# A hybrid decoder block on one core: gates computed ahead of the branch projections, the projections in seven block products, and a written instruction order

## The chip, the core and the metric

One core of a Trainium2 chip runs the whole block in one launch. The metric is device time in microseconds (us). TensorE (PE) multiplies, VectorE (DVE), ScalarE (ACT) and GpSimd (POOL) work elementwise, SyncE (SP) issues most DMAs.

## The reference

1024 tokens and 16 meta tokens, width 1024, fp32. Three mixers read one normalised input; their outputs are projected, gated and merged, then come an output projection, a residual and a squared-ReLU MLP. What is computed after the mixers:

```python
g = sigmoid(gates).reshape(b, l, 3, 1024)          # gates = h @ w_in[:, 9216:12288]
merged = (g[:, :, 0] * (ret @ w_branch[0]) + g[:, :, 1] * (diff @ w_branch[1])
          + g[:, :, 2] * (conv @ w_branch[2]))
x = x + merged @ w_out
u = square(relu(rms_norm(x, norm2_w) @ w_up))      # 1024 -> 4096
return x + u @ w_down                              # then the final rms_norm
```

## The kernel before

Tokens lie along the free dimension, channels on the 128 partitions. A matrix product works on tiles of 128 output channels (f) by 512 tokens (a half, j). Each fp32 operand is split into a high part hi (a cast to fp32r) and a rest lo = x - hi (`split`, L135 and L136); each 128-deep step of a product is three matmuls: hi.hi, hi.lo, lo.hi (`kstep`, L161 to L163; `product`, L858 to L860). The hi part of a weight is copied on ACT, the lo part is subtracted on POOL.

**Mixers.** Retention, differential attention and the convolution are woven together; each leaves its output, by tiles of channels, in DRAM: `rT`, `dT`, `cT`.

**Gates and branches (L690 to L740).** For each of the three branches, in the order conv, attention, retention: the 8 operand tiles are loaded and split into the slots that the mixers left (L714). For each f, the gate columns of `w_in` are multiplied with H, the normalised input, scaled (L250, DVE) and put through a sigmoid (L704, ACT); two gates run ahead of the branch product. The product of the branch with its `w_branch` tile takes 8 steps of three matmuls a half; DVE multiplies it with the gate and adds it to the merged tile M (L736 to L739). Then M is split.

**Output projection (L758 to L776).** For each half and f: 24 matmuls, the residual is added (L766), the sum stored to DRAM, squared on ACT (L769) and summed over f on DVE (L773). Ones times that sum (L775) gives the sum of squares for all partitions; `rstd_from` (L188 to L192) makes the scale R2 of it with two ACT and three DVE operations.

**Up and down projections (L777 to L1014).** Here products are made of seven block products (Strassen-Winograd). A pair of f tiles, split in K and in N, is a 2 x 2 of blocks; the right operand's seven blocks are B11, B21, T1 = B12 - B11, B22, T2, T3 and T4, each kept as hi and lo in eight and six buffers of SBUF (`opnd`). The weight's seven left blocks are made from four loaded blocks by four DVE sums a pair (`comb`, L825) and split on ACT and POOL. Two pairs (four f) run together in `block_products`: seven times 2 x 4 x 3 = 24 matmuls, with the copies of finished banks on ACT (L869). The right blocks of the up projection come from X2 by `normalise` (L908) and `sums` (L929). The results U are squared ReLUs (L966, L967), their seven blocks go to DRAM. The down projection sums over 32 tiles of U in blocks of 16, 16, 16 and 8 by pairs; `right_ops` (L1006) loads seven blocks ahead of each and splits them, alternating POOL and DVE; `down_use` adds the residual on POOL (L1012) and the product on DVE (L1013). The last four tiles of U go through plain matmuls in `last_down` with the final norm, the tail.

The order of instructions on each engine is planned by the framework from dependencies and priorities; weights have high priority. Within an engine everything runs in that order. SP issues every load and nearly every store, also in order.

Memory: one stack of pools. `cp`, `xp` (tags C and R) and `sm` stay to the end; the others are closed behind the output projection, and the pools of the up and down projections take their place.

Of the kernel before, what the change touches and what calls it, by code (L numbers as in the profile page):

```python
# [12 lines left out]
F32 = mybir.dt.float32  # L13
# [58 lines left out]
def trunk_kernel(ctx: ExitStack, tc, x, w_in, w_branch, w_out, w_up, w_down, w_down2, w_down3, vecs, lam_in, consts, y):  # L72
    nc = tc.nc
    PSUM = bass.MemoryType.PSUM
    early = ExitStack()
    cp = ctx.enter_context(tc.tile_pool(name="cp", bufs=1))
    xp = ctx.enter_context(tc.tile_pool(name="xp", bufs=1))
    sm = ctx.enter_context(tc.tile_pool(name="sm", bufs=6))
    ap = early.enter_context(tc.tile_pool(name="ap", bufs=1))
    wp = early.enter_context(tc.tile_pool(name="wp", bufs=3))  # L80
    sp = early.enter_context(tc.tile_pool(name="sp", bufs=1))
    ps = early.enter_context(tc.tile_pool(name="ps", bufs=1, space=PSUM))
# [4 lines left out]
    def slot(tag, shape, dt=F32):  # L87
        uid[0] += 1
        return (xp if tag in ("C", "R") else sp).tile(shape, dt, tag=tag, bufs=SLOTS[tag], name=f"{tag}{uid[0]}")
# [176 lines left out]
    dT = [dram([P, SEQ]) for _ in range(KT)]  # L266
    cT = [dram([P, SEQ]) for _ in range(KT)]
    rT = [dram([P, SEQ]) for _ in range(KT)]
# [78 lines left out]
    def diff_attn(h, ops):  # L347
# [102 lines left out]
        nc.gpsimd.dma_start(out=dT[h], in_=o32)  # L450
# [19 lines left out]
    def conv_out(f, u):  # L470
# [3 lines left out]
        for c0, w in CH_TOK:  # L474
# [8 lines left out]
            if c0 != META:  # L483
                nc.gpsimd.dma_start(out=cT[f], in_=yt)
# [49 lines left out]
    def ret_gate(h, yt):  # L534
        for z in range(2):
            wt = weights(w_in[G_RG + 2 * h + z])
            for c0, w in CH_TOK:
# [8 lines left out]
                if c0 != META:  # L546
                    nc.gpsimd.dma_start(out=rT[2 * h + z], in_=yt[z])
# [142 lines left out]
    turns[:] = TURNS  # L690
    last_sig = [None]
    M = [None] * KT
    otags = ["Q"] * 4 + ["B"] * 4 + ["S"] * 2 + ["A"] * 6
    for br, src in ((2, cT), (1, dT), (0, rT)):
        def gate(f):
            if f >= KT:
                return None
            wt = weights(w_in[G_GATE + br * KT + f])
            out = []
            for c0, w in CH_TOK:  # L700
                pt = gemm(wt, H, c0, w)
                gt = slot("t2", [P, 512])
                scaled(gt, pt, c0, w)
                sig = a.activation(out=gt, in_=gt, func=AF.Sigmoid)  # L704
                last_sig[0] = sig
                out.append(gt)
            return out
        O = []

        def operands(ks):  # L710
            for k in ks:
                oh = slot(otags[2 * k], [P, SEQ], F32R)
                ol = slot(otags[2 * k + 1], [P, SEQ], F32R)
                nc.sync.dma_start(out=f32(ol), in_=src[k])  # L714
                for j in range(2):
                    c = slice(j * 512, (j + 1) * 512)
                    split(f32(ol[:, c]), oh[:, c], ol[:, c])
                O.append((oh, ol))

        gq = [gate(0)]  # L720
        operands(range(0, 4))
        gq.append(gate(1))
        operands(range(4, 8))
        for f in range(KT):
            gts = gq[f]
            wt = weights(w_branch[br * KT + f])
            if M[f] is None:
                M[f] = slot("C", [P, SEQ])
            if f == KT - 1:
                pts = gemm2(wt, O)  # L730
            else:
                pts = [gemm(wt, O, i * 512, 512) for i in range(2)]
            for i, pt in enumerate(pts):
                mc = M[f][:, i * 512:(i + 1) * 512]
                if br == 2:
                    v.tensor_tensor(out=mc, in0=pt, in1=gts[i], op=ALU.mult)  # L736
                else:
                    v.tensor_tensor(out=gts[i], in0=pt, in1=gts[i], op=ALU.mult)
                    v.tensor_tensor(out=mc, in0=mc, in1=gts[i], op=ALU.add)  # L739
            gq.append(gate(f + 2))  # L740


    with tc.issue_after(getattr(last_sig[0], "ins", last_sig[0])):
        a.preload_act_table_set("natural_log_exp_and_others")
    MO = []
    for k in range(KT):
        mh = slot("H", [P, SEQ], F32R)
        ml = slot("H", [P, SEQ], F32R)
        split(M[k], mh, ml)
        MO.append((mh, ml))  # L750

    X2 = [None] * KT
    xd = [dram([P, SEQ]) for _ in range(KT)]
    R2 = slot("R", [P, SEQ])
    for i in range(2):
        c = slice(i * 512, (i + 1) * 512)
        acc = None
        for f in range(KT):  # L758
            wt = weights(w_out[f])
            if X2[f] is None:  # L760
                X2[f] = slot("C", [P, SEQ])
            uid[0] += 1
            raw = wp.tile([P, HW], F32, tag="raw", name=f"xr{uid[0]}")
            nc.sync.dma_start(out=raw, in_=x[:, f, META + i * 512:META + i * 512 + 512])
            pt = gemm(wt, MO, i * 512, 512)
            v.tensor_tensor(out=X2[f][:, c], in0=pt, in1=raw, op=ALU.add)  # L766
            nc.sync.dma_start(out=xd[f][:, c], in_=X2[f][:, c])
            sq = slot("t2", [P, 512])
# [39 lines left out]
    def row_ops(srcs, cols):  # L808
# [18 lines left out]
        with tc.high_priority():  # L827
            a11 = [load(s[0]) for s in srcs]
            for p in range(n):
                op(0, a11[p])  # L830
# [317 lines left out]
```

## Time and profile before

| what | value |
|---|---|
| median of 3 runs | 2437.56 us (2434.89 to 2437.66) |
| the profiled execution, its own time | 2437.59 us |
| its span, first to last instruction | 2435.8 us |
| mean granted TensorE clock | 0.986 of full speed |
| bytes moved by DMA | 209.56 MB, 86 GB/s |

Times in the trace count from the span's start. A matmul's recorded duration overlaps the next one's, since they are pipelined; the rate of a stretch is read from the number of matmuls in it. The granted clock 1.00 is 2.4 GHz, 0.50 is 1.2 GHz.

### The profile page before, as it was taken

What the parts mean: (1) busy time and instruction counts of PE and PEld (TensorE: products, weight loads), DVE (VectorE), ACT (ScalarE), POOL (GpSimd) and SP (SyncE); (2) the same over time, 40 slices, a digit from 0 to 9 for tenths busy, and PEclk for the clock granted to TensorE, in tenths of its full rate; (3) what the DMA queues carried; (4) which work ended last, traced back from release to release, by engine and by line L of the source; (5) the groups of instructions that cost most, each with busy time, mean ns of one, the idle gap of its engine ahead of it and who ended that gap; (6) DMA issues with size and microseconds to landing.
All of it is one profiled execution on the core that took longest, in us unless ns stands there. A gap on an engine that the chain in (4) does not pass through costs nothing. (4 is left out here: it accounts for less than half of the span.)

```text
span 2435.8 us, 32151 instructions
## 1 busy us (share of the span) xinstructions
PE 2338.4 (96%) x11994; PEld 2021.5 (83%) x11994; DVE 1393.6 (57%) x2639; ACT 956.7 (39%) x1867; POOL 961.2 (39%) x768
## 2 busy tenths in 40 slices
PE   8999999999999999999999999998599999989897
PEld 7999999999999989988888888876478887767777
DVE  7776777776765676671122232244676668656545
ACT  6554554554543333341131131132333335344344
POOL 2233223222222211222222222233765557898894
PEclk9999999999999999999999999999799999999999
DMA  3111111111111111131131131134245356434221
GB/s 136 35 53 44 44 53 44 44 53 44 44 53 39 54 56 53 52 128 56 44 120 44 49 116 48 48 96 153 71 139 173 131 163 251 177 117 156 96 95 70
DMA packets 96300, 209.56 MB, mean 86 GB/s; under 512 B 10640, under 2 KB 14864, under 8 KB 93456
## 3 DMA queue, kind: packets, MB, share of 16 engines
q1 hardware_dynamic: 92688, 194.92, 23.1%
q0 software_dynamic: 3456, 12.58, 1.3%
q8 instruction: 94, 1.54, 0.3%
q14 instruction: 62, 0.51, 0.1%
HBM read 158.71 MB, written 48.76 MB: 85 GB/s over the span
## 5 line engine op out<-in xcount | busy, mean ns | idle before, releaser
L136 POOL TENSOR_TENSOR wlo<-raw,whi 128x512 fp32r<-128x512 f32 x270 | 367.6, 1363 | 1071.5 <-ACT whi L135 997.1
L161 PE MATMUL pmm<-H,whi 128*128 128x512 f32 (+3 forms) x1704 | 598.1, 353 | 9.7 <-ACT H L196 7.1
L163 PE MATMUL pmm<-H,wlo 128*128 128x512 f32 (+3 forms) x1704 | 598.5, 352 | 3.6 <-POOL wlo L136 3.6
L162 PE MATMUL pmm<-H,whi 128*128 128x512 f32 (+3 forms) x1704 | 598.3, 352 | 2.2 <-DVE H L197 2.2
L136 POOL TENSOR_TENSOR w<-raw,w 128x512 fp32r<-128x512 f32 (+1 forms) x224 | 310.3, 1396 | 152.5 <-ACT w L135 151.8
L858 PE MATMUL pb<-op,w 128*128 128x512 f32 x840 | 331.2, 398 | 39.4 <-ACT w L135 31.8
L161 PEld LDWEIGHTS pmm<-H,whi 128*128 128x128 f32 x1704 | 320.6, 189 | 39.6 <-ACT H L196 7.1
L163 PEld LDWEIGHTS pmm<-H,wlo 128*128 128x128 f32 x1704 | 320.9, 188 | 32.8 <-POOL wlo L136 6.6
L135 ACT CAST whi<-raw 128x512 fp32r<-128x512 f32 x272 | 168.7, 621 | 453.7 <-PE pmm L162 154.9
L162 PEld LDWEIGHTS pmm<-H,whi 128*128 128x128 f32 x1704 | 321.1, 189 | 30.0 <-DVE H L197 3.2
L859 PE MATMUL pb<-op,w 128*128 128x512 f32 x840 | 332.6, 396 | 8.9 <-DVE op L136 6.9
L860 PE MATMUL pb<-op,w 128*128 128x512 f32 x840 | 324.6, 396 | 12.3 <-POOL w L136 12.1
L135 ACT CAST w<-raw 128x512 fp32r<-128x512 f32 (+1 forms) x224 | 131.2, 595 | 319.5 <-PE pb L860 176.2
L858 PEld LDWEIGHTS pb<-op,w 128*128 128x128 f32 x840 | 161.4, 192 | 78.0 <-ACT w L135 35.1
L825 DVE TENSOR_TENSOR raw<-raw,raw 128x512 f32<-128x512 f32 (+1 forms) x128 | 144.4, 1150 | 105.5 <-POOL w L136 52.0
L860 PEld LDWEIGHTS pb<-op,w 128*128 128x128 f32 x840 | 160.0, 191 | 52.7 <-POOL w L136 19.6
L859 PEld LDWEIGHTS pb<-op,w 128*128 128x128 f32 x840 | 161.0, 192 | 43.7 <-DVE op L136 7.6
L250 DVE TENSOR_TENSOR t<-pmm,R 128x512 f32<-128x512 f32 (+2 forms) x60 | 36.8, 619 | 85.5 <-PE pmm L163 85.4
L380 ACT ACTIVATE B<-B,nb 128x144 f32<-128x144 f32 (+3 forms) x64 | 50.7, 792 | 85.5 <-DVE nb L379 85.2
L704 ACT ACTIVATE t<-t 128x512 f32<-128x512 f32 x48 | 30.4, 633 | 123.2 <-DVE t L250 122.1
L135 ACT CAST op<-op 128x512 fp32r<-128x512 f32 x106 | 58.6, 619 | 37.9 <-DMA op<-d 37.6
L371 PE MATMUL ps<-A,Q 128*128 128x256 f32 (+6 forms) x224 | 72.3, 327 | 0.3 <-DVE mx L374 0.3
(336 smaller groups left out, 4301.3 us busy)
## 6 DMA issues: line engine op xcount, KB each, us to landing
raw<-w_in SPq DMA_DIRECT2D x192, 256.0 KB, 2.5
d<-C SPq DMA_DIRECT2D x122, 256.0 KB, 3.0
op<-d SPq DMA_DIRECT2D x21, 1024.0 KB, 5.7
raw<-w_up SPq DMA_DIRECT2D x64, 256.0 KB, 2.9
raw<-w_down SPq DMA_DIRECT2D x56, 256.0 KB, 2.8
raw<-w_branch SPq DMA_DIRECT2D x48, 256.0 KB, 2.6
d<-C POOLq DMA_DIRECT2D x16, 512.0 KB, 3.0
raw<-w_out SPq DMA_DIRECT2D x32, 256.0 KB, 3.2
```

The source lines that it names most:

```text
L135: a.copy(out=hi, in_=src)
L136: (eng or v).tensor_tensor(out=lo, in0=src, in1=f32(hi), op=ALU.subtract)
L161: nc.tensor.matmul(pt, lhsT=hi[:, s], rhs=xh[:, c0:c0 + w], start=start, stop=False)
L162: nc.tensor.matmul(pt, lhsT=hi[:, s], rhs=xl[:, c0:c0 + w], start=False, stop=False)
L163: nc.tensor.matmul(pt, lhsT=lo[:, s], rhs=xh[:, c0:c0 + w], start=False, stop=stop)
L250: v.tensor_tensor(out=out, in0=pt, in1=R[:, c0:c0 + w], op=ALU.mult)
L371: nc.tensor.matmul(sps[:, 0:cw], lhsT=q[m][:, qc], rhs=kk[m][:, c], start=True, stop=False)
L380: a.activation(out=pt, in_=pt, func=AF.Exp, scale=slope, bias=nb, accum_out=st[:, m:m + 1])
L825: v.tensor_tensor(out=dst, in0=x0, in1=x1, op=o)
L858: nc.tensor.matmul(pt, lhsT=w[0][:, s], rhs=b[0][:, k], start=first, stop=False, skip_group_check=True)
L859: nc.tensor.matmul(pt, lhsT=w[0][:, s], rhs=b[1][:, k], start=False, stop=False, skip_group_check=True)
L860: nc.tensor.matmul(pt, lhsT=w[1][:, s], rhs=b[0][:, k], start=False, stop=k == nk - 1, skip_group_check=True)
```

## The change

The 24 gate tiles are computed ahead of all branches, in one loop that the framework still orders; the sigmoids are stored to DRAM (`GD`) by POOL's queue. In the same loop, from the third gate tile on, the sums T1 to T4 of the branch outputs are made and stored to DRAM (`TD`), and the first four right blocks of the first branch are loaded and split.

From there on the work is a list of steps: 42 for the branches (three branches, two quads of four f, seven products), 16 for the output projection, 56 for up and 56 for down. Each step has a load (issued three steps ahead), a preparation of its weights (two steps ahead), its matmuls in two parts, and an evacuation of each part; further tables place the splitting of right blocks, loads and stores at steps. The main loop at the end writes all engines' instructions in this order, and the framework keeps it.

Per step a `Quad` runs one of the seven products for two pairs: 24 matmuls. Weight lo parts go three in four to POOL, one to DVE (`WLO`). Right blocks are split by `build`: copies three in four on ACT, one on DVE; lo parts three in four on DVE, one on POOL. Right blocks of the next set are loaded in steps 1 to 7 and split in steps 3 to 9 counted from the last quad of the current set (`turn_over`). In the output projection lo parts alternate between POOL and DVE, and the sum of squares moves from DVE to POOL. The merging of branches and the residual adds of the down projection alternate between POOL and DVE. The up projection begins with products 1 and 2 of its first two quads; its seven right blocks follow one a step.

Pools stand on two stacks. On the left `cp`, and above it the mixers' pools (with tag C), which close ahead of the gates and give way to `pa` (eight right-block buffers) and `mp` (weights). On the right H, R, the temporaries and the gates' weights, which close ahead of the steps and give way to `pb` (six buffers) and `mq` (rings: kept banks 6, gates 3, X 16). The eight PSUM banks are one ring from the first step on. `last_down` keeps its work. The core of the diff:

```diff
-    early = ExitStack()
+    mixers, gates = ExitStack(), ExitStack()
...
+    RING = {"raw": 10, "w": 5, "t": 6, "g": 3, "k": 2, "X": 16}
...
-    for br, src in ((2, cT), (1, dT), (0, rT)):
-        def gate(f):
...
-            if f == KT - 1:
-                pts = gemm2(wt, O)
-            else:
-                pts = [gemm(wt, O, i * 512, 512) for i in range(2)]
...
+    for n, (br, f) in enumerate((br, f) for br, _ in BR for f in range(KT)):
+        wt = weights(w_in[G_GATE + br * KT + f])
+        for c0, w in CH_TOK:
+            pt = gemm(wt, H, c0, w)
+            gt = slot("t2", [P, 512])
+            scaled(gt, pt, c0, w)
+            last_sig = a.activation(out=gt, in_=gt, func=AF.Sigmoid)
+            nc.gpsimd.dma_start(out=GD[br][:, f, c0 - META:c0 - META + w], in_=gt)
+        if n >= 2 and sums_todo and n != 14:
+            branch_sums(*sums_todo.pop(0))
+        if n == 14:
...
+        def op(self, i, p, src):
+            w = temp("w", [P, 2, 512], F32R)[:, :, 0:self.nk * P]
+            a.copy(out=w[:, 0], in_=src)
+            lo_part("w", self.lo_engines, src, w[:, 0], w[:, 1])
...
+    def build(src, oh, ol, key="set"):
+        e = pick(key + "c", (a, a, a, v))
+        if e is a:
+            a.copy(out=oh, in_=src)
+        else:
+            v.tensor_copy(out=oh, in_=src)
+        lo_part(key + "l", (v, v, v, G), src, oh, ol)
...
+            at(fetch, L + i + 1, load)
+            at(work, L + i + 3, split_op)
...
+                if sb is not None:
+                    v.tensor_tensor(out=sb, in0=pt, in1=sb, op=ALU.add)
...
+                    v.tensor_tensor(out=g, in0=pt if sb is None else sb, in1=g, op=ALU.mult)
+                    pick("m", (G, v)).tensor_tensor(out=M[f, j], in0=M[f, j], in1=g, op=ALU.add)
+
+            for s, (r, j) in ((-1, (0, 0)), (2, (0, 1)), (4, (1, 1)), (5, (1, 0))):
+                at(fetch, L + s, lambda r=r, j=j, fn=gate_load: fn(r, j))
...
+    mid = {S0 + 9: lambda: token_scale(0), E0: lambda: token_scale(1)}
...
+    at(work, E0 + 1, lambda: up_t1(range(2)))
+    at(work, E0 + 2, lambda: up_t1(range(2, 4)))
+    at(work, E0 + 3, lambda: plain_op("B22", range(4)))
+    at(work, E0 + 4, lambda: up_sum("T2", (1, 1), (1, 1), (0, 1)))
+    at(work, E0 + 5, lambda: up_sum("T3", (0, 0), (1, 1), (0, 0)))
+    at(work, E0 + 6, lambda: up_sum("T4", (1, 0), (1, 0), (1, 1)))
...
+    with tc.manual_schedule():
+        for s in range(-LL, N + 2):
+            now[0] = s
+            if 0 < s <= N:
+                steps[s - 1][3](1)
+            for fn in soon.get(s, ()):
+                fn()
+            if 0 <= s + LP < N:
+                steps[s + LP][1]()
+            if 0 <= s < N:
+                steps[s][2](0)
+                if s in mid:
+                    mid[s]()
+                steps[s][2](1)
+                steps[s][3](0)
+            for fn in work.get(s, ()):
+                fn()
+            for fn in fetch.get(s, ()):
+                fn()
+            if 0 <= s + LL < N:
+                steps[s + LL][0]()
```

## Rows read from the trace of the kernel before

**Rows 1.** The page: busy us, share of the span and instructions.

```profile
PE 2338.4 (96%) x11994; PEld 2021.5 (83%) x11994; DVE 1393.6 (57%) x2639; ACT 956.7 (39%) x1867; POOL 961.2 (39%) x768
```

**Rows 2.** Stages: length, PE, PEld, DVE, ACT, POOL busy, PE clock, DMA share, GB/s.

```profile
0.00:1076.20 1076.20, 1064.40 (x6484) 993.36 (x6485) 752.13 (x1903) 512.05 (x1077) 270.45 (x275) 1.00 0.16 56
1076.20:1608.60 532.40, 532.40 (x2304) 431.57 (x2303) 138.34 (x197) 118.19 (x191) 127.02 (x99) 1.00 0.19 67
1608.60:1725.10 116.50, 98.06 (x390) 71.98 (x388) 45.07 (x50) 36.03 (x61) 44.92 (x33) 0.97 0.48 152
1725.10:2063.10 338.00, 315.61 (x1345) 257.57 (x1346) 245.19 (x263) 129.28 (x231) 213.29 (x135) 0.95 0.43 148
2063.10:2388.80 325.70, 293.58 (x1249) 235.85 (x1248) 184.63 (x178) 140.57 (x266) 288.93 (x215) 0.97 0.36 128
2388.80:2435.80 47.00, 34.37 (x229) 31.13 (x227) 28.20 (x52) 20.61 (x44) 16.54 (x14) 0.88 0.26 90
```

**Rows 3.** Busy time in three single stretches, same columns.

```profile
1725.00:1735.00 10.00, 5.00 (x10) 2.98 (x10) 10.00 (x7) 1.60 (x4) 8.96 (x6) 0.50 0.14 54
1800.00:2000.00 200.00, 200.00 (x884) 165.59 (x883) 132.77 (x151) 71.83 (x126) 107.77 (x74) 1.00 0.46 154
2065.00:2070.00 5.00, 4.89 (x21) 4.05 (x22) 4.54 (x4) 3.62 (x8) 5.00 (x4) 1.00 1.00 409
```

**Rows 4.** Waits of PE, 1608.6 to 2388.8: us in total, times, longest.

```profile
PE pb L858 <- ACT w L135: 31.8, 6, 7.4
PE pb L860 <- POOL w L136: 12.1, 13, 3.9
```

**Rows 5.** Timeline where the up stage begins: start, us, instruction, idle before.

```profile
1717.86 1.13 PE L775 MATMUL po<-t,onesr 128*128 128x512 f32 x2 [2.17 <-DVE t L773]
1724.48 1.64 DVE L908 SCALAR_TENSOR_TENSOR C<-C,vec,R 128x512 f32<-128x512 f32 x1
1725.09 0.80 PE L858 MATMUL pb<-op,w 128*128 128x512 f32 x1 [6.11 <-ACT w L135]
```

**Rows 6.** Lines 136 and 478: ns shortest/median/longest, first and last start.

```profile
L136 POOL TENSOR_TENSOR op<-op,op x42: 1272/1732/1822, 2035.3 to 2257.2; 128x512 fp32r<-128x512 f32 x42
L136 DVE TENSOR_TENSOR op<-op,op x42: 673/1744/1803, 2036.4 to 2257.7; 128x512 fp32r<-128x512 f32 x42
L478 DVE TENSOR_SCALAR C<-C,vec x16: 481/488/1514, 124.9 to 789.7; 128x512 f32<-128x512 f32 x16
```

**Rows 7.** Timeline of POOL and DVE, 1734 to 1770, neighbours merged.

```profile
1737.17 13.05 POOL L136 TENSOR_TENSOR op<-t,op 128x512 fp32r<-128x512 f32 x1 [3.20 <-ACT op L135]
1746.60 2.48 DVE L929 TENSOR_TENSOR C<-C 128x512 f32<-128x512 f32 x4
1756.31 10.15 POOL L136 TENSOR_TENSOR op<-C,op 128x512 fp32r<-128x512 f32 x6
1756.82 3.48 DVE L929 TENSOR_TENSOR C<-C,C 128x512 f32<-128x512 f32 x2
```

**Rows 8.** Groups of instructions, whole span: count, busy us, mean ns, idle before.

```profile
L869 ACT COPY t<-pb 128x512 f32<-128x512 f32 x96 | 55.7, 581 | 2.6 <-PE pb L860 2.6
L1013 DVE TENSOR_TENSOR C<-pb,t 128x512 f32<-128x512 f32 x48 | 32.2, 684 | 31.8 <-POOL t L1012 21.9 <-PE pb L860 9.7
```

**Rows 9.** The page: DMA issues, count, KB each, us to landing.

```profile
op<-d SPq DMA_DIRECT2D x21, 1024.0 KB, 5.7
raw<-w_up SPq DMA_DIRECT2D x64, 256.0 KB, 2.9
```

**Rows 10.** Instructions on the DRAM buffers: issuing a DMA on POOL, ns.

```profile
L450 POOL DMA_DIRECT2D d<-C x8: 533/573/573, 168.4 to 803.3; - x8
```

**Rows 11.** Busy time of L136 alone in the down stage: DVE, POOL.

```profile
2063.10:2388.80 325.70, 64.43 (x45) 219.55 (x163) 0.97 0.36 128
```

**Rows 12.** Groups of instructions in the down stage, columns as rows 8.

```profile
L825 DVE TENSOR_TENSOR raw<-raw,raw 128x512 f32<-128x512 f32 (+1 forms) x62 | 76.2, 1254 | 61.2 <-POOL w L136 30.8 <-DMA raw<-w_down 30.0
L1012 POOL TENSOR_TENSOR t<-t,C 128x512 f32<-128x512 f32 x48 | 68.2, 1422 | 0.0
```

More of the change, by code (lines that the diff above doesn't have):

```diff
@@ L743, in trunk_kernel @@
[L743 to L768, printed above, removed]
-            a.activation(out=sq, in_=X2[f][:, c], func=AF.Square)
-            if acc is None:
-                acc = sq
-            else:
-                v.tensor_tensor(out=acc, in0=acc, in1=sq, op=ALU.add)
-        ssq = bank("o")
-        nc.tensor.matmul(ssq, lhsT=ones, rhs=acc, start=True, stop=True)
-        rstd_from(ssq, D, R2[:, c], slot("t2", [P, 512]))
@@ L854, in product @@
-    def product(pt, w, b, nk, more):
-        for k in range(nk):
-            s = slice(k * P, (k + 1) * P)
-            first = k == 0 and not more
-            nc.tensor.matmul(pt, lhsT=w[0][:, s], rhs=b[0][:, k], start=first, stop=False, skip_group_check=True)
-            nc.tensor.matmul(pt, lhsT=w[0][:, s], rhs=b[1][:, k], start=False, stop=False, skip_group_check=True)
-            nc.tensor.matmul(pt, lhsT=w[1][:, s], rhs=b[0][:, k], start=False, stop=k == nk - 1, skip_group_check=True)
@@ new lines, in trunk_kernel, with acc_bank, at @@
+    gates.close()
+    pb = ctx.enter_context(tc.tile_pool(name="pb", side="right", **reuse))
+    mq = ctx.enter_context(tc.tile_pool(name="mq", side="right", **reuse))
+    p8 = ctx.enter_context(tc.tile_pool(name="p8", space=PSUM, **reuse))
+    def acc_bank():
+        uid[0] += 1
+        return p8.tile([P, 512], F32, tag="b", bufs=8, name=f"pb{uid[0]}")
+    LP, LL = 2, 3
+    steps = []
+    work = {}
+    fetch = {}
+    soon = {}
+    def at(table, s, fn):
+        table.setdefault(s, []).append(fn)
@@ new lines, in trunk_kernel, with load, split_op, merged @@
+    for i, name in enumerate(ORDER[4:]):
+        def load(name=name):
+            open_op(SET, name, 4, False)
+            nc.sync.dma_start(out=f32(SET[name][1]), in_=right_src(2, name))
+        def split_op(name=name):
+            for k in range(4):
+                build(f32(SET[name][1][:, k]), SET[name][0][:, k], SET[name][1][:, k])
+        at(fetch, -1, load)
+        at(work, 2 + i, split_op)
+    MO = {}
+    KO = (0, 1, 2, 3, 4, 6, 5, 7)
+    def merged(f, js):
+        if f not in MO:
+            MO[f] = opnd(True, [P, 2, SEQ])
+        for j in js:
+            build(M[f, j], MO[f][:, 0, half(j)], MO[f][:, 1, half(j)])
@@ L955, in store, with use @@
                 if p0 <= pair < p0 + n:
[L956 to L961 removed]
+                    put(UD[b][name][:, pair - p0, :], src)
+        def use(p, r, j, pt, sb):
+            u = U[r, j] = temp(FIRST_U[pair] if pair < 4 and (r, j) == (0, 0) else "X", [P, 512])
             if sb is None:
```

567 lines of the change are left out of this document (333 added, 234 removed).

## The prediction

> **What bounds the kernel now.** I began with the page's busy shares: TensorE is busy 96% of the span, no other engine over 57% [rows 1]. An average hides stages, so next came the busy time by stage [rows 2]. The reader should see two halves. Up to 1608.6 us PE never idles (532.40 of 532.40 us in the gate and branch stage): there, only fewer or shorter matmuls can help. From 1608.6 to 2388.8 us PE is short of work: 18.4 us idle in the output projection, 22.4 in the up stage, 32.1 in the down stage.
>
> Busy time is not the right measure of what each stage could do, so I count matmuls. 2304 in 532.4 us is 231 ns each in the gate and branch stage; in a full stretch of the up stage 884 in 200 us is 226.6 ns (two at an edge may count twice) [rows 2, 3]. At 226.6 ns the 384 of the output stage would take 87.2 us (it takes 116.5), the 1344 of the up stage 304.5 (338.0) and the 1176 of the down stage 266.5 (325.7): 29.3, 33.5 and 59.2 us, 122 us in all, are idle time or half clock. The half clock is real but small: after a wait of 6 us the clock stood at 0.50 (1.2 GHz) for a whole 10 us stretch [rows 3, 5].
>
> What PE waits for is a weight operand: the hi half from ACT (31.8 us), whose copy waits for a block sum on DVE, or the lo half from POOL (12.1) [rows 4]. So DVE and POOL are behind the stalls. Neither is full on its own (DVE 184.6 and POOL 288.9 of 325.7 us in the down stage [rows 2]), but they get in each other's way. The same lo subtraction takes 1.27 us at least on POOL and 1.73 in the middle; on DVE 0.67 and 1.74 [rows 6]. When both queue, six POOL ops take 10.15 us and two DVE ops 3.48: they alternate, 1.69 to 1.74 us a pair [rows 7]. A DVE op alone with a queue behind it takes 0.62 (four in 2.48); so I charge 0.62 us for a DVE op with two SBUF inputs and 1.07 for a POOL op, against one common account, the **pair**. DVE ops that read PSUM stay at 0.684 us on average, with POOL 89% busy [rows 2, 8], and are not charged. The account can also be won outright by one side: while DVE ran some twenty such ops in a row, one POOL op lasted 13.05 us [rows 7].
>
> **The change, part by part.**
>
> *Fewer products.* Three branches now take 8 x 2 x 8 x 3 = 384 matmuls each; seven products of 4 x 4 x 3 = 48 make 336. 144 fewer. The gates stay 1152 at 231 ns, 266.2 us. The branch products take the form of the up stage (one bank, weights and operands in the same layout), so I price them at its 226.6 ns: 1008 x 0.2266 = 228.4 us; at 231 ns it would be 4.4 us more. Together 494.6 instead of 532.4: **37.8 us** less, on the path, because PE is full there.
>
> *Gates first.* Each of 48 sigmoid halves is now stored by POOL's DMA queue and read back by SP; 48 more POOL stores carry the branch sums. A POOL DMA issue takes 0.57 us [rows 10], 96 of them 55 us, beside 48 lo subtractions at 1.27, 61 us: 116 of 266 us. The 48 new DVE sums are 30 us. The cover is 266 us of gate matmuls that need none of it; without the cover the 55 us would delay lo halves one for one. I charge nothing.
>
> *Hand-over.* T2, T3 and T4 of the first branch go into memory that H holds until the last gate matmul, so their loads (1 MB each) queue SP, and behind them stand four weight blocks of product 3. A 1 MB load lands in 5.7 us [rows 9]; the best stretch moved 409 GB/s [rows 3], so 4.5 MB is some 11 us, then sum, copy and lo, 3 us: about 14 us against 10.9 us of products 1 and 2. Charged 4 us (0 to 12).
>
> *Branch stage.* The pair's account for six quads of four output tiles. Weight lo halves: 84, three in four on POOL, 0.75 x 1.07 + 0.25 x 0.62 = 0.96, 80.6 us. Block sums 48 x 0.62 = 29.8. Product times gate where the sum lies in SBUF, 36 x 0.62 = 22.3. Merges for two branches, 32, half each, x 0.845 = 27.2. Operand splits: 56 for the next branches, 12 for T2 to T4, 10 of the merged result, 78 in all; lo three in four on DVE is 0.73, and every fourth copy is a DVE copy. DVE shows no such copy; the nearest row is a one-input op of 512 columns, 0.488 us [rows 6], and its charge lies between nothing and that. I take all of it, 0.12 a split: 78 x 0.85 = 66.3. Sum 226 us for 228.4 us of matmuls. For the fill I price before's down stage alike: POOL has 163 subtractions [rows 11], of which 45 are operand splits (DVE has 45 too), 8 the last weights and 110 weight lo, 28 of them half as wide, so 96; then 48 residual adds and 62 block sums, 16 of them half as wide [rows 12]. 96 x 1.07 + 48 x 1.07 + 45 x (1.07 + 0.62) + 54 x 0.62 + 8 x 1.07 = 272 us in 325.7, a fill of 0.84, with POOL itself 89% busy [rows 2]. After the change POOL has far fewer ops, so I take 0.90; bounds 0.84 and 1. 226 / 0.90 = 251 us: **23 us of stall** (0 to 41). Here most of the gain of 37.8 us is given back; what is late is the weight lo behind operand splits. ACT is no bound: two copies, one keep and three operand copies a step, at 0.6, make 3.6 of 5.4 us [rows 8].
>
> *Output stage.* 87.2 us of matmuls; the account holds 32 lo halves and 12 adds, about 40 us with the splits. Loads come three steps (16 us) ahead. What remains is the merged operand of the last product and its chain of multiply, merge, copy, lo, some 4 us, with 18 matmuls (4.1 us) ahead of it. 3 us (0 to 15); 26 us won of 29.3.
>
> *Up stage.* The second half's scale took 6.6 us from its sums (1717.86) to the first use (1724.48) [rows 5], bare; now four products that need only the first half cover it, 21.8 us. But then T1, B22, T2, T3 and T4 must follow one a step: normalise, combine and split, 8.4 + 5.9 + 17.6 = 31.9 us of the account, on top of 3.2 us a step for weights, sums and squared ReLU. Eight steps last 43.5 us and ask for 57.5: 14 us over. Then about 4 at the end, where the down operands are split, and 4 for the clock: **22 us** (6 to 33.5, all that is lost now).
>
> *Down stage.* Weight lo 98 (in units of 512 columns) x 0.96 = 94.1; sums 56 x 0.62 = 34.7; residual adds 48 x 0.845 = 40.6; splits 82 x 0.85 = 69.7; last operands 14.5: 254 us for 266.5 of matmuls. 254 / 0.90 = 282, **15 us of stall** (0 to 35) in place of 59.
>
> *Two stacks of pools, order of steps.* Mixers (1076.2 us) and tail (47.0) keep their work. The written order has its price in the waits above, and in rival C.
>
> *Sum.* 1076.2 + 270.2 + 251.3 + 90.2 + 326.5 + 281.8 + 47.0 = 2343.2 us of span. The profiled run took 2437.59 with a span of 2435.8, 1.8 outside; 2437.59 is the median, 2437.56. So **2345 us**, 3.8% less.
>
> The Trainium skill, in SBUF — State Buffer, section Who interferes with whom, states that a DVE instruction with two SBUF inputs and a GpSimd one that reads SBUF exclude each other for the whole instruction. By that rule a pair would cost the durations that each has alone. The trace agrees that they exclude each other, but a pair costs 1.69 to 1.74 us, not 0.67 + 1.27 = 1.94 [rows 6, 7].
>
> **The rivals.**
>
> *A. The order hides nearly everything* (0.22). The account never goes over, because splits are done four steps before they are used. All stages at their matmuls plus about 20 us: 1076.2 + 266.2 + 228.4 + 87.2 + 304.5 + 266.5 + 47 + 1.8 = 2278, so 2290 to 2315. For: seen over whole stages the account just fits, 226 of 228 and 254 of 266 us. Against: in the steps with splits it wants 7 of 5.4 us, and one POOL op was shut out for 13 us [rows 7].
>
> *B. The pair is dearer than I charge* (0.18). Its fill stays at before's 0.84: branch 269, down 302, up as badly off as now, 338: 18 + 20 + 11 over my sum, 2394 us. Charged at lone durations (0.68 and 1.28) the accounts are 257 and 291 us; with a fill of 0.95, 270 and 306 us, 2389. Of the 0.18, 0.06 is for this second way. The rule of the Trainium skill (SBUF — State Buffer, Who interferes with whom) names the second way. Against it stand the pairs of 1.69 to 1.74 us [rows 7].
>
> *C. Slower: the written order locks the step* (0.04). SP issues in order: gate loads have three buffers and wait for a product's evacuation, stores wait for sums, and weight loads stand behind both. If a load then lands after DVE has come to its block sum, DVE blocks, and with it the evacuation of the next product. There are 42 + 16 + 56 + 56 = 170 steps; the gain over my floor is 2437.6 - 2278 = 160 us, so it decides from 0.94 us a step. At half a landing of 2.9 us [rows 9] each step would lose 1.45 us: 2525 us. Against: loads are issued three steps ahead.
>
> *D. Gain given back* (0.01). The stalls add up to all 160 us: no change.
>
> **How the numbers follow.** My forecast (2320 to 2375) has 0.55. The range runs from 2295 (most of A) to 2400 (most of B) and leaves out C, D, and the ends of A and B, under 2 in 10. Three runs of before span 0.11%, so 0.2% (4.9 us) is about what can be told from no change; faster by more than that is all of A, B and the forecast: 0.95; same 0.01; slower 0.04.
>
> **What would show it.** Right: gates near 266 us with PE full; branch products at 227 ns, in about 251 us; no wait over 4 us in the output stage; the longest remaining idle at the head of the up stage, ended by ACT or POOL weight operands; DVE two-input ops still between 0.68 and 1.75 us. Wrong: a branch stage over 270 us, or waits of PE or DVE ended by DMA landings step after step (C); a PE without gaps in the branch and down stages (A).

## The result and the profile after

The changed kernel takes **2457.91 us** (median of four runs, 2457.13 to 2458.72); the kernel before, measured beside it, 2437.61 (2434.89 to 2438.26). The ratio is 1.0085, 95% interval 1.0068 to 1.0103: **slower by 0.85%**, where 3.8% less was forecast, and outside the range. The profiled run has a span of 2455.3 us, 112.1 more than the 2343.2 of my sum.

First the page of the changed kernel (busy us, share, instructions), which answers to [rows 1].

```profile
PE 2330.6 (95%) x11854; PEld 2009.7 (82%) x11854; DVE 1570.2 (64%) x2963; ACT 987.6 (40%) x1929; POOL 918.4 (37%) x804
```

PE has 140 instructions fewer, about the 144 that went, and DVE has 177 us more to do. Neither says where the time went. The stages do (columns as [rows 2]; in order mixers, gates, branches, output, up, down, tail):

```profile
0.00:1080.70 1080.70, 1065.95 (x6483) 995.28 (x6484) 747.53 (x1913) 504.66 (x1065) 266.37 (x275) 1.00 0.15 52
1080.70:1349.60 268.90, 266.55 (x1154) 215.63 (x1152) 93.59 (x112) 69.03 (x117) 126.22 (x155) 1.00 0.60 211
1349.60:1654.70 305.10, 255.62 (x1008) 201.06 (x1009) 206.36 (x244) 99.34 (x179) 142.87 (x96) 0.92 0.40 138
1654.70:1748.40 93.70, 91.12 (x389) 73.46 (x388) 47.12 (x58) 34.36 (x59) 43.90 (x33) 0.98 0.55 177
1748.40:2094.30 345.90, 323.47 (x1349) 259.54 (x1348) 245.73 (x307) 129.89 (x222) 138.90 (x95) 0.96 0.48 158
2094.30:2407.10 312.80, 292.19 (x1237) 233.01 (x1236) 199.81 (x276) 126.32 (x240) 179.48 (x136) 0.99 0.36 130
2407.10:2455.30 48.20, 35.72 (x242) 31.76 (x240) 30.04 (x55) 23.97 (x49) 20.63 (x17) 0.91 0.25 88
```

Against my sum: mixers +4.5, gates with the hand-over -1.3, branch stage **+53.8** (305.1 for 251.3), output +3.5, up **+19.4** (345.9 for 326.5), down and tail together **+32.2** (361.0 for 328.8). PE is idle 49.5 us in a branch stage that before the change had no gap at all [rows 2], and the half clock comes with it (a granted clock of 0.92 over the stage). The half clock has a price of its own: at the rates that e4 shows below, the 1008 matmuls would take some 231 us at full clock, so I estimate that some 20 of the 255.62 busy us are lost to it. What PE waits for is new. The waits of PE (us in total, times, longest):

```profile
PE pb L850 <- DVE t L934: 31.7, 7, 5.3
PE pb L850 <- ACT t L859: 29.5, 12, 6.3
PE pb L850 <- DVE X L1170: 16.6, 8, 4.0
...
PE pb L852 <- POOL w L793: 2.8, 4, 0.9
```

Those of ACT and DVE for the branch weights, and those of SP in the branch stage:

```profile
ACT w L820 <- DMA raw<-w_branch: 74.7, 18, 10.6
DVE raw L826 <- DMA raw<-w_branch: 38.2, 7, 13.0
...
SPq L928 <- POOL X L940: 143.1, 13, 18.5
SPq L928 <- DVE X L937: 69.3, 13, 16.0
SPq L928 <- DVE X L940: 27.6, 8, 5.9
```

Before, PE waited for weight operands, hi and lo [rows 4]. Now it waits for **evacuations**: for the sum that empties a bank (L934, L1170) and for ACT's copy of a bank (L859). A product that goes on in the bank of the one before it (4 after 3, 6 after 5, 7 after 6) can't start until that bank is read, and the other half of the step, 2.7 us (12 x 0.2266), is all the time there is. And SP stands 240 us in the branch stage (143.1 + 69.3 + 27.6) before gate loads, each waiting until a product consumes the gate whose buffer it takes. Behind them stand the weight loads, for which ACT and DVE wait 112.9 us. One such case, timelines of SP, ACT, DVE and PE of the changed kernel:

```profile
1467.39 16.98 SPq L928 DMA_DIRECT2D g<-d  x3
1484.77 0.81 SPq L808 DMA_DIRECT2D raw<-w_branch  x2
...
1487.79 0.62 ACT L820 CAST w<-raw 128x512 fp32r<-128x512 f32 x1 [7.06 <-DMA raw<-w_branch]
1489.14 0.62 ACT L820 CAST w<-raw 128x512 fp32r<-128x512 f32 x1 [0.73 <-DMA raw<-w_branch]
...
1489.79 0.69 DVE L793 TENSOR_TENSOR w<-raw,w 128x512 fp32r<-128x512 f32 x1 [4.50 <-ACT w L820]
1490.40 0.68 DVE L934 TENSOR_TENSOR t<-pb,t 128x512 f32<-128x512 f32 x1
...
1491.14 0.79 PE L850 MATMUL pb<-op,w 128*128 128x512 f32 x1 [4.98 <-DVE t L934]
```

Three gate loads hold SP from 1467.39 to 1484.37, and only behind them, at 1484.77, are the weights issued. ACT's copy waits 7.06 us for them, DVE's lo half 4.50 us for that copy, and only then comes the evacuation L934, which stands behind the lo half in the order written for DVE. PE waits 4.98 us to begin product 7, for weights of a step that it will come to later.

### The profile page after: what moved, and what is told of

Same layout as the page of the kernel before. It is cut to its first block, busy times and chain, and to the rows that moved or that the text cites. A ratio compares the mean times of both kernels' runs of the same rounds, so it can differ in the third digit from the quotient of the medians.

```text
span 2455.3 us, 32724 instructions
## 1 busy us (share of the span) xinstructions
PE 2330.6 (95%) x11854; PEld 2009.7 (82%) x11854; DVE 1570.2 (64%) x2963; ACT 987.6 (40%) x1929; POOL 918.4 (37%) x804
## 3 DMA queue, kind: packets, MB, share of 16 engines
q1 hardware_dynamic: 111840, 231.63, 27.6%
## 5 line engine op out<-in xcount | busy, mean ns | idle before, releaser
L161 PE MATMUL pmm<-H,whi 128*128 128x512 f32 (+3 forms) x1640 | 574.3, 352 | 14.2 <-ACT H L196 8.5
L162 PE MATMUL pmm<-H,whi 128*128 128x512 f32 (+3 forms) x1640 | 574.0, 351 | 1.6 <-DVE H L197 1.5
L850 PE MATMUL pb<-op,w 128*128 128x512 f32 x1176 | 480.1, 408 | 89.0 <-DVE t L934 31.7
L136 POOL TENSOR_TENSOR wlo<-raw,whi 128x512 fp32r<-128x512 f32 x190 | 256.7, 1352 | 638.1 <-ACT whi L135 590.1
L852 PE MATMUL pb<-op,w 128*128 128x512 f32 x1176 | 473.3, 403 | 2.9 <-POOL w L793 2.8
L851 PE MATMUL pb<-op,w 128*128 128x512 f32 x1176 | 473.3, 402 | 1.2 <-POOL op L793 1.2
L820 ACT CAST w<-raw 128x512 fp32r<-128x512 f32 (+1 forms) x308 | 181.9, 601 | 502.7 <-DVE raw L826 218.8
L850 PEld LDWEIGHTS pb<-op,w 128*128 128x128 f32 x1176 | 228.6, 194 | 156.6 <-ACT t L859 36.7
L852 PEld LDWEIGHTS pb<-op,w 128*128 128x128 f32 x1176 | 228.3, 194 | 58.2 <-POOL w L793 5.1
L851 PEld LDWEIGHTS pb<-op,w 128*128 128x128 f32 x1176 | 229.0, 195 | 52.5 <-POOL op L793 1.5
L135 ACT CAST whi<-raw 128x512 fp32r<-128x512 f32 x192 | 118.6, 619 | 193.6 <-PE pmm L162 70.7
L793 DVE TENSOR_TENSOR w<-raw,w 128x512 fp32r<-128x512 f32 (+1 forms) x92 | 87.2, 948 | 138.7 <-ACT w L820 98.2
L793 DVE TENSOR_TENSOR op<-op,op 128x512 fp32r<-128x512 f32 x114 | 101.4, 941 | 30.9 <-ACT op L889 30.9
L859 ACT COPY t<-pb 128x512 f32<-128x512 f32 x132 | 75.8, 582 | 44.1 <-PE pb L852 43.8
L793 POOL TENSOR_TENSOR op<-op,op 128x512 fp32r<-128x512 f32 x38 | 56.2, 1480 | 88.9 <-DVE op L891 79.6
```

The costliest lines, as they stand in the source:

```text
L135: a.copy(out=hi, in_=src)
L136: (eng or v).tensor_tensor(out=lo, in0=src, in1=f32(hi), op=ALU.subtract)
L161: nc.tensor.matmul(pt, lhsT=hi[:, s], rhs=xh[:, c0:c0 + w], start=start, stop=False)
L162: nc.tensor.matmul(pt, lhsT=hi[:, s], rhs=xl[:, c0:c0 + w], start=False, stop=False)
L793: pick(key, engines).tensor_tensor(out=lo, in0=src, in1=f32(hi), op=ALU.subtract)
L820: a.copy(out=w[:, 0], in_=src)
```

## The experiments

All twelve were measured beside the kernel before; ratios are to that. Lengths of stages in us, from the busy time by stage.

| run | median us | ratio (95%) | branch | up | down + tail |
|---|---|---|---|---|---|
| changed kernel | 2457.91 | 1.0085 (1.0068 to 1.0103) | 305.1 | 345.9 | 361.0 |
| e1 weight loads first | 2411.09 | 0.9872 (0.9856 to 0.9887) | 259.0 | 345.9 | 362.9 |
| e2 products reordered | 2442.77 | 1.0007 (0.9997 to 1.0017) | 280.1 | 341.2 | 364.0 |
| e3 both | 2401.84 | 0.9842 (0.9827 to 0.9856) | 246.8 | 340.6 | 366.2 |
| e4 address only | 2456.64 | 1.0069 (1.0052 to 1.0086) | 308.6 | 342.0 | 360.0 |
| e5 gate loads behind | 2420.24 | 0.9914 (0.99 to 0.9929) | 268.6 | 344.8 | 363.9 |
| e6 e3, bank copy first | 2392.24 | 0.9804 (0.9788 to 0.9821) | 252.8 | 339.1 | 350.6 |
| e7 e1, bank copy first | 2402.66 | 0.9841 (0.9827 to 0.9856) | 257.2 | 343.4 | 361.8 |
| e8 no written order | 2390.72 | 0.9791 (0.9776 to 0.9805) | 256.4 | 332.8 | 366.9 |
| e9 e8, products reordered | 2374.66 | 0.973 (0.9716 to 0.9745) | 246.8 | 332.4 | 357.3 |
| e10 e9 and address | 2368.32 | 0.9704 (0.9687 to 0.972) | 245.9 | 327.4 | 353.7 |
| e11 e8, lo halves shared | 2389.72 | 0.9791 (0.9777 to 0.9806) | 254.1 | 334.3 | 364.5 |
| e12 e10, three quads open | 2364.97 | 0.9692 (0.9675 to 0.9708) | 246.0 | 323.9 | 354.0 |

**e1, weight loads first.** In the loop over steps, the weights of the step three ahead are issued before the step's other loads and stores.

```
-            for fn in fetch.get(s, ()):
-                fn()
             if 0 <= s + LL < N:
                 steps[s + LL][0]()
+            for fn in fetch.get(s, ()):
+                fn()
```

> SP issues the weight loads of a step ahead of that step's gate loads, stores and right-block loads, nothing else changes. Theory L (weight loads stand behind gate loads that wait for one of three buffers): the waits for landing w_branch tiles go (74.7 us on ACT and 38.2 us on DVE in the changed kernel), the branch stage falls from 305 to under 270 us and the whole by 35 us or more. Theory E (evacuations are late: a product that goes on in the bank of the product before it has half a step, 2.7 us, for the evacuation, which stands in the written order behind preparations and splits): the waits for landing go too, since they are one thing that holds DVE up, but PE's waits for DVE and ACT evacuations at the fourth and seventh product stay; the branch stage falls by 10 to 25 us, up and down by under 3. Theory P (DVE and POOL together are full): less than 5 us.

Measured: 2411.09 us, branch stage 259.0 for 305.1, up, down and tail as they were: theory L's case. The waits for w_branch are all but gone, and with them nearly two thirds of those for L934. The waits of ACT, DVE and PE in this run:

```profile
ACT w L820 <- DMA raw<-w_branch: 9.4, 3, 3.7
DVE raw L826 <- DMA raw<-w_branch: 5.8, 3, 2.4
...
PE pb L850 <- DVE t L934: 11.7, 6, 2.9
```

This one exchange turns a loss of 0.85% into a gain of 1.3%. SP's order is the largest cause, and only in the branch stage. SP itself still waits 189 us there for gate buffers (240 in the changed kernel), but no weight load of the same step stands behind those waits any more.

**e2, products reordered.** The seven products of a quad run in the order 1, 3, 5, 4, 6, 2, 7, so that no product goes on in the bank of the one just before it; the sums, kept banks and operand splits are moved to fit. The first two quads of the up stage keep the old order.

```
+        SEQ = (0, 2, 4, 3, 5, 1, 6)
...
-            for i in range(7):
+            for i in Quad.SEQ:
                 product_step(q, i)
```

> The seven products in the order 1, 3, 5, 4, 6, 2, 7 (the first two quads of the up projection keep theirs), so that between two products in one bank there is always one in another bank, and an evacuation has a step and a half (8 us) in place of half a step (2.7 us). Same matmuls, same elementwise work. Theory E: PE's waits for evacuations (44 us of its waits in the branch stage, 20 in the down stage) nearly go; branch stage 305 to 255 to 270 us, down stage 313 to 295, up stage by 3 to 10 us (its worst part is in the quads that keep the order), whole 2458 to 2385 to 2400. Theory L: the weights are as late as before and PE then waits for them, branch stage above 290, whole above 2440. Theory P: the waits end on lo halves of weights instead, branch stage above 285.

Measured: 2442.77 us, not theory E's 2385 to 2400. The branch stage loses 25 us, to 280.1, between the ranges of theory E (255 to 270) and theory L (above 290). The down stage stays at 312.3, where theory E said 295. The output stage is 8.8 us longer, and the tail 3.5, which is work: 257 matmuls for 242. So the half step of slack is a second cause, smaller than SP's order. It costs little without the written order: the kernel before has the same products in the same banks in its up and down stages, and the largest of its PE's waits for evacuations there are:

```profile
PE pb L858 <- ACT t L869: 3.5, 2, 2.2
PE pb L858 <- DVE C L1013: 2.9, 2, 2.3
```

**e3, both.**

> Both edits. Theory E with L as a helper: branch stage 240 to 260 us, whole 2370 to 2390, some 10 us under the product order alone. Theory L alone: as the first run. Theory P: above 285 us in the branch stage whatever the order.

Measured: 2401.84 us, 12 over theory E's range; the branch stage of 246.8 is within its 240 to 260, and under the 251.3 of the prediction. What is left is ACT's bank copy, L869 in this kernel. The largest of PE's waits:

```profile
PE pb L860 <- ACT t L869: 34.5, 22, 6.2
```

One case in the down stage, timelines of ACT, DVE and PE in this run:

```profile
2129.73 1.22 ACT L826 CAST w<-raw 128x512 fp32r<-128x512 f32 x2 [4.51 <-DVE raw L832]
2130.85 0.58 ACT L869 COPY t<-pb 128x512 f32<-128x512 f32 x1
...
2128.21 2.01 DVE L832 TENSOR_TENSOR raw<-raw,raw 128x512 f32<-128x512 f32 x2
2131.98 2.72 DVE L793 TENSOR_TENSOR op<-op,op 128x512 fp32r<-128x512 f32 x3 [1.77 <-ACT op L903]
...
2131.48 0.50 PE L860 MATMUL pb<-op,w 128*128 128x512 f32 x1 [1.62 <-ACT t L869]
```

ACT's bank copy stands behind weight copies that wait 4.51 us for a block sum on DVE; then DVE waits 1.77 us for operand copies that stand behind the bank copy on ACT. Both queues are written, and each waits for the other while neither is full.

**e4, address only.** The rate of the matmuls differed by operand, and the operands' addresses do too: this run puts an unused tile of 1056 bytes before the right-hand operands, so that their address has the same remainder by 2048 as that of the weights.

```
+    pad = ctx.enter_context(tc.tile_pool(name="pad", side="right", **reuse))
+    pad.tile([P, 264], F32, tag="pad", name="pad0")
     pb = ctx.enter_context(tc.tile_pool(name="pb", side="right", **reuse))
```

> An unused 1056-byte tile below the right stack of the steps, so that right operands in pb start at the same remainder of 2048 bytes (960) as those in pa and as the weights; before it the remainder was 2016. In the changed kernel products with operands in pa run at 226.7 ns a matmul and those with operands in pb at 233.4, three of seven products. Theory: relative placement of weight and operand sets the rate; all products at 227 ns, 10 us less of PE time, 5 to 10 us less in all. Rival: something else than placement (which bank, which order): products with operands in pb stay at 233 ns, same time within 3 us.

Measured: these matmuls start every 226.7 ns in place of 233.4. The first and the last of 24 in a row (product 5 of the first quad), in the changed kernel:

```profile
1377.18 0.40 PE L850 MATMUL pb<-op,w 128*128 128x512 f32 x1
...
1382.55 0.40 PE L852 MATMUL pb<-op,w 128*128 128x512 f32 x1
```

The same matmuls in this run:

```profile
1377.05 0.39 PE L852 MATMUL pb<-op,w 128*128 128x512 f32 x1
...
1382.26 0.39 PE L854 MATMUL pb<-op,w 128*128 128x512 f32 x1
```

The rate is the theory's (23 intervals in 5.21 us for 5.37), but its 5 to 10 us less are not there. The time doesn't move (2456.64 us): what PE wins is waited away, up -3.9 us, branch +3.5.

**e5, gate loads behind.** Of SP's entries only the gate loads go behind the weights; the 1 MB loads and the stores stay ahead.

```
-                at(fetch, L + s, lambda r=r, j=j, fn=gate_load: fn(r, j))
+                at(behind, L + s, lambda r=r, j=j, fn=gate_load: fn(r, j))
...
                 steps[s + LL][0]()
+            for fn in behind.get(s, ()):
+                fn()
```

> The changed kernel with one edit: on SP, only the loads of the gate halves (48, 0.25 MB each) are put behind the weight loads of their step; the 1 MB loads of the next operands and the stores stay ahead of them. Theory C (a gate load waits for its buffer until a product is evacuated, and the weight loads queue behind it): the branch stage falls from 305.1 to some 260 to 268 us, as it did to 259.0 with all loads behind the weights; about 2418 us. Rival (the 1 MB loads and the bandwidth they take hold the weights): branch stage at 290 us or over, about 2445 us or more. Up and down stages as in the changed kernel (346, 313) by both, since their fetch entries are untouched.

Measured: branch stage 268.6 us, 36.5 of the 46.1 of e1, just over the 260 to 268 of theory C and far from the rival's 290. The gate loads are what holds the weights; the other entries add some 10 us.

**e6, bank copy first.** On top of e3: block sums stay ahead of the step, the weight copies and lo halves go behind the evacuation of the first half.

```
                 steps[s][3](0)
+                if s + LP < N:
+                    steps[s + LP][4]()
```

> The third experiment (weight loads first, products in the order 1 3 5 4 6 2 7) with one more edit: the block sums for the step after next stay ahead of the step, but ACT's weight copies and the lo halves come behind the evacuation of the step's first half, so that ACT's copy of a finished bank no longer stands behind copies that wait for sums on DVE. Coupling theory (ACT and DVE, each in its written order, wait for each other): PE's waits for ACT's bank copy (34.5 us in 22 waits in the third experiment) fall to 15 or less, the down stage from 312.2 to 295 to 303, up from 340.7 to 328 to 336, about 2375 to 2390 us. Rival P (POOL and DVE are full by their common account): waits only change their name, to lo halves, and the time stays within 0.4% of 2402.

Measured: 2392.24 us, 2 over the range of the coupling theory; down 295.5 as it said, up 339.1 and not 328 to 336. The bank copy's waits fall to 19.6 us, not 15, and 17.5 us of waits for POOL's lo halves appear; the branch stage grows from 246.8 to 252.8 us. The waits of PE in this run:

```profile
PE pb L863 <- ACT t L872: 19.6, 5, 6.9
PE pb L865 <- POOL w L793: 17.5, 13, 3.0
```

The coupling is real; what gets out of its way delays the weights instead.

**e7, bank copy first, old product order.** The same split on top of e1.

> The first experiment (weight loads first, the change's own product order) with the split preparation of the run before. By the half-step theory the stalls at the products that go on in the same bank come from the evacuation having only half a step (2.7 us); if what delays it is ACT's queue, this alone takes most of them: PE's waits for bank copies and for DVE's evacuations (28.9, 16.4 and 11.7 us) fall by half or more, 2385 to 2395 us. If DVE's own queue delays it, DVE's share of the waits stays (28 us) and the time is 2398 to 2412 us. Rival P: no change from 2411.

Measured: 2402.66 us. ACT's part of the waits falls from 28.9 to 20.0 us, DVE's hardly (13.4 + 12.8 for 11.7 + 16.4): the second case, DVE's evacuations are late by DVE's own queue.

**e8, no written order.** The line that fixes the order is taken out; operations, engines and buffers stay.

```
-    with tc.manual_schedule():
+    with nullcontext():
         for s in range(-LL, N + 2):
```

> The changed kernel with the same operations on the same engines, but without the written order: the scheduler of the framework orders the queues from its own costs and priorities, as it did before the change. If the written order is what costs (theory C with its waits), the branch stage falls well below 305 us and the time comes under 2430 us. Rival (the work itself, the pair account, is too much for these stages, whatever the order): 2445 to 2475 us, with waits spread over other operands.

Measured: **2390.72 us**, 2.1% faster than before, and under the 2430 of the first theory. The same work in the order of the framework's scheduler takes 67 us less than in the written one. PE's waits for evacuations are nearly gone (4.9 + 2.2 + 1.6 us for 77.8 in the changed kernel), and what I had expected, waits for weight operands, stands at the head of the list. The waits of PE in this run:

```profile
PE pb L850 <- ACT w L820: 22.8, 7, 4.5
PE pb L852 <- POOL w L793: 9.3, 5, 4.3
...
PE pb L850 <- DVE X L1170: 4.9, 5, 1.3
...
PE pb L850 <- ACT t L859: 2.2, 3, 1.3
...
PE pb L850 <- DVE t L934: 1.6, 1, 1.6
```

One case in the down stage, timeline of all engines:

```profile
2126.29 4.18 DVE L793 TENSOR_TENSOR op<-op,op 128x512 fp32r<-128x512 f32 x5
...
2132.20 0.68 DVE L826 TENSOR_TENSOR raw<-raw,raw 128x512 f32<-128x512 f32 x1
...
2132.99 1.66 ACT L820 CAST w<-raw 128x512 fp32r<-128x512 f32 x3 [7.62 <-DVE raw L826]
...
2134.18 0.79 PE L850 MATMUL pb<-op,w 128*128 128x512 f32 x1 [3.74 <-ACT w L820]
```

DVE does five operand splits in 4.18 us, the block sums for product 4 come after them, ACT's copy waits 7.62 us for a sum and PE 3.74 for the copy.

**e9, reordered products without the written order.**

> The changed kernel without the written order and with the products in the order 1 3 5 4 6 2 7 (the edits of the second and the eighth experiment together). In the eighth the longest waits left are at the fourth product of a quad (3.6 to 4.7 us, seven times, some 28 us): products 3 and 4, side by side, want six of a quad's eight block sums on DVE, with operand splits between them. Theory (DVE's order of sums and splits sets these waits): product 5, which needs no sum of its own, now stands between 3 and 4, so the waits at product 4 fall to half or less: 2372 to 2384 us. Rival (the pair account is full in these stages): the waits move to other products and the time stays within 0.3% of 2390.7.

Measured: 2374.66 us, within the theory's range: with product 5 between products 3 and 4, the stalls at product 4 come to 9.8 us in the timeline (six, in the down stage), where e8 has 25.7 in seven by the same count, over the branch and down stages.

**e10, and the address.**

> The kernel of the run before with the unused 1056-byte tile of the fourth experiment, which puts the right-hand operands at the same remainder of their address as the weights. Matmuls with these operands run at 226.7 in place of 233.4 ns (shown in the fourth experiment, where the time was waited away). 3 of 7 products in 3528 matmuls are 1512, at 6.7 ns each 10.1 us at most. If PE is now the bound in most steps: 5 to 10 us less than the run before. If other engines set the step: within 2 us of it.

Measured: 2368.32 us, 6.3 less (2365.61 to 2370.48 against 2373.92 to 2376.15). A full stretch of 100 us in the up stage, busy time as in [rows 3], first in e9:

```profile
1850.00:1950.00 100.00, 100.00 (x436) 81.44 (x435) 68.79 (x86) 35.61 (x62) 41.76 (x27) 1.00 0.47 159
```

The same stretch in e10:

```profile
1850.00:1950.00 100.00, 100.00 (x442) 82.79 (x442) 67.69 (x84) 36.99 (x65) 42.00 (x28) 1.00 0.48 163
```

That is 442 matmuls for 436. So the rate that e4 won for nothing counts once PE is the bound in most steps.

**e11, lo halves shared equally.** On top of e8.

```
-    WLO = (G, G, G, v)
+    WLO = (G, v)
```

> The kernel of the eighth experiment (no written order) with the weights' lo halves shared equally, POOL and DVE in turn, instead of three in four on POOL. By my account of the pair (0.62 us for a DVE op, 1.07 for a POOL op, one common account) this is cheaper: a quarter of some 290 lo halves by 0.45 us, 33 us of account over branch, up and down: if the account is what fills up, the time falls by 8 to 25 us, to 2366 to 2383. If DVE's own queue is what is late (block sums and evacuations behind its splits), it gets more to do and the time rises by 3 to 20 us, to 2394 to 2411.

Measured: 2389.72 us, no change: neither theory. POOL has 112.7 us less to do (852.0 for 964.7 in the span) and DVE 20.2 more, and the time doesn't notice. So the account is not what fills these stages as a whole. Where it bites is in a burst. Line 793 in this run, ns shortest/median/longest:

```profile
L793 POOL TENSOR_TENSOR w<-raw,w x170: 736/1302/13979, 1212.2 to 2323.8; 128x512 fp32r<-128x512 f32 x156, 128x256 fp32r<-128x256 f32 x14
```

Timelines of POOL and DVE near the head of the up stage:

```profile
1730.30 15.21 POOL L793 TENSOR_TENSOR w<-raw,w 128x512 fp32r<-128x512 f32 x2 [4.95 <-ACT w L820]
...
1730.04 2.48 DVE L1082 TENSOR_TENSOR X<-X,X 128x512 f32<-128x512 f32 x4
...
1735.46 0.41 DVE L891 CAST op<-X 128x512 fp32r<-128x512 f32 x1
...
1738.20 3.09 DVE L793 TENSOR_TENSOR op<-X,op 128x512 fp32r<-128x512 f32 x5
```

While DVE runs ops with two SBUF inputs back to back, at 0.62 us each (2.48 for four, 3.09 for five), two POOL ops take 15.21 us, much as one took 13.05 in [rows 7], and PE's longest wait for a lo half of POOL is 9.4 us. The Trainium skill (SBUF — State Buffer, Who interferes with whom) says that the two exclude each other for a whole instruction and that the order of issue decides who blocks; the trace agrees that POOL is blocked, but through a whole run of DVE instructions, a copy among them, and not through one.

**e12, three quads open.** On top of e10, three quads of the up stage run products 1 and 2 before any runs its third.

```
-    for q, i in [(q, i) for q in range(2) for i in range(2)] + [(q, i) for q in range(2) for i in range(2, 7)] + \
-            [(q, i) for q in range(2, 8) for i in Quad.SEQ]:
+    for q, i in [(q, i) for q in range(3) for i in range(2)] + [(q, i) for q in range(3) for i in range(2, 7)] + \
+            [(q, i) for q in range(3, 8) for i in Quad.SEQ]:
```

> The kernel of the tenth experiment with one edit in the up stage: three quads, not two, run their products 1 and 2 before any runs its third, so T1, B22, T2, T3 and T4 have two steps (10.9 us) more until they are used. At the head of the up stage the tenth lost some 15 us in four waits and 3 to 5 at half clock. My account of that head (eight steps ask for 57.5 of 43.5 us): with ten steps it asks for 63.9 of 54.4, so 9.5 us of the 14 stay, and the time falls by 4 to 5 us. Rival (only the time until first use is short, the engines are not full): these waits go to 4 us or less, 10 to 16 us less time, 2352 to 2358 us. Third possibility: the third quad's early weights hold buffers that others wait for, and nothing is won.

Measured: 2364.97 us, 3.4 less than e10, but the runs of the two overlap (2364.07 to 2371.16 against 2365.61 to 2370.48), so the third possibility, that nothing is won, is not excluded. In the profiled runs the up stage is 3.5 us shorter, under the account's 4 to 5 and far from the rival's 10 to 16. Two of the waits left there are ended by operand copies on ACT (7.4 us in two), so the account's mechanism is not shown. It has the lowest median of all, 3.1% under the kernel before (interval 2.9 to 3.3%).

## Why the prediction was wrong

**What held.** Seven products for eight save what they should: 1008 matmuls in place of 1152. Gates first cost nothing: 266.55 of 268.90 us busy in their stage. The output stage came to 93.7 us for 90.2 (88.8 with the weight loads first).

**The step that failed** is the last line on the parts: "The written order has its price in the waits above, and in rival C". I charged the order nothing of its own. Nearly every wait of my sum was one for a full pair of engines, and the written order makes waits between engines that are not full. e8 measures it: 67 us by the medians. By the spans it is 64.1 us: the order costs 48.7 in the branch stage, 13.1 in the up stage, 4.4 in the mixers and 4.3 in the output stage, and wins 0.5 in the gates and 5.9 in down and tail. How it reaches the mixers, which the framework orders in both, no run shows. Without the written order the time is inside my range, and the span is 48.0 us over my sum: 16.5 are the term of the down stage below, 25.4 go with the product order and the address (e9, e10), and 6.1 are left.

**Rival C was the largest part of it, at 0.04.** It named the queue, the gate loads with three buffers and the weight loads behind them, and both of its signs came: a branch stage over 270 us, and waits ended by landings of weights (18 on ACT, 7 on DVE). My argument against it, "loads are issued three steps ahead", fails because SP waits up to 18.5 us for one gate buffer, more than three steps of 5.4. Its account was wrong too: 1.45 us a step over 170 steps, where e1 shows 46.1 us over the 42 steps of the branch stage, 1.10 a step, and nothing in the up and down stages, which have no gate loads. So it did not need all 170 steps: 46 us, added to the rest of the miss, was enough to change the sign.

**What I did not see at all** is the half step. I looked at which operands come late and not at which banks must be free: products 4, 6 and 7 go on in the bank of the product before. The written orders of DVE and ACT put weight work for two steps ahead, and operand splits, in front of the evacuation. In the branch stage the new order of products takes 25.0 us off (e2), or 12.2 where the loads are mended already (e1 to e3); in down and tail it wins nothing alone (361.0 to 364.0, e2), but 11.2 once the bank copy comes first (361.8 to 350.6, e7 to e6).

**Down stage, a term mis-sized by 16.5 us.** I counted 1176 matmuls against 325.7 us and called 59.2 us lost. But [rows 2] show 1249 in that stage: 73 belonged to the last block, done early in the gaps, and 73 x 0.2266 = 16.5 us were work. Down and tail together hold 1478 matmuls before (1249 + 229) and 1479 after (1237 + 242, one at an edge), so my 328.8 us should have been 345.3. e6 comes to 350.6.

**Up stage, 19.4 us over.** 13.1 of it is the written order (e8), 0.4 the product order (e9), 5.0 the rate of matmuls with right-hand operands (e9 to e10), which I had priced at 226.6 ns throughout; with all three, e10 stands at 327.4 us for my 326.5. That the end agrees does not show that each wait in my working was right: the 14 us that I charged at the head are there (four waits of some 15 us in e10), the rest is not told apart.

**The pair's account.** My branch stage of 251.3 us, made from it, lies between e1 (259.0) and e3 (246.8). Yet e11 took some 33 us off that account and won nothing, so the agreement is not evidence for its fill of 0.90. Rival B, which differs from the forecast by that fill, argued about a quantity that did not decide here.

**What stays open.** Which of the waits left in e12 can be taken out: some 18 us of gaps in the down stage (295.3 us with 277.6 busy), and 11 in the up stage (323.9 with 313.0). Nor did I try the written order with DVE's block sums and operand splits behind the evacuations as well.

## What to carry to other kernels

A written order is a cost term of its own: for every engine ask of each instruction what it may wait for and who stands behind it, and put loads that wait for a buffer behind loads that don't, on the same queue. Before costing throughput, count the time from the end of one use of a PSUM bank to the next, and put evacuations ahead of work for later steps. When a stage's floor is taken from its matmuls, take the count that the trace shows in that stretch, since other work may be filling the gaps.

## What the runs showed of the hardware

The rate of a matmul depends on where its operands lie. The addresses here are those at which the kernel's pools place the buffers of an operand. With the buffers of the moving operand and of the weights at the same remainder of their address by 2048 bytes (960 and 960) matmuls of 512 columns start every 226.7 ns; with 2016 against 960, every 233.4 ns, 3% more, at full clock and without any wait. Moving the right-hand operands by 1056 bytes took the difference away, in e4 and again in e10. The kernel before has operands and weights of its up and down stages at one remainder (928) and runs at 226.6 there [rows 3]; in its gate and branch matmuls, at 231 [rows 2], they differ, but there nothing was moved. Which other remainders are slow, whether 2048 is the unit that counts, and why, no run here shows.

A copy of 128x512 on DVE from SBUF takes 0.41 us, not the 0.488 that I took from a one-input op with a constant [rows 6].
